# A two-layer hybrid diffusion backbone: attention by pairs of heads, and other places for modulation and stage ends

## The chip, the core and the metric

The kernel runs on one core of a Trainium2 chip. The metric is device time in microseconds (us) of one execution. Three runs gave 1413.24, 1419.32 and 1423.5 us; the median is 1419.32.

## What is computed

The reference is one inference step of two layers (`DEPTH`) over 128 context tokens and 256 latent tokens with 1024 channels. Cut to what matters:

```python
def _block(x, mod, lw, mix):
    g = lw['norm_g']
    h = _rms(x, g[0]) * (1 + mod[:, None, 1]) + mod[:, None, 0]
    y, aux = mix(h)
    x = x + mod[:, None, 2] * _rms(y @ lw['w_out'], g[1])
    h = _rms(x, g[2]) * (1 + mod[:, None, 4]) + mod[:, None, 3]
    f = jnp.square(jax.nn.relu(h @ lw['ffn_w1'])) @ lw['ffn_w2']
    x = x + mod[:, None, 5] * _rms(f, g[3])
    return x, aux
def _modulation(cond, w, b):
    m = jax.nn.silu(cond) @ w + b          # six vectors of 1024 for each layer
    return m.reshape(cond.shape[0], N_MOD, D_MODEL)
# mix: h @ w_in is cut into four groups of heads
#   A bidirectional RWKV-7 (a recurrence), B neighbourhood attention, C bidirectional HGRN2, D windowed attention with a sink
#   y = concat(A, B, C, D); attention for one query block:
    p = jax.nn.softmax(jnp.concatenate([s_loc, s_ctx], axis=-1), axis=-1)
    o = jnp.einsum('bhrcqak,brackhd->brcqhd', p_loc, vb) + jnp.einsum('bhrcql,blhd->brcqhd', p_ctx, cv)
...
```

B and D have four heads of 64 channels each. Context queries see context only, latent queries see latent and context.

## The kernel before

All 384 tokens lie in three tiles of 128 partitions, or, transposed, as 128 channels by 384 tokens. Weights come in units of 128x1024 (512 KB). A dense product is made in three passes over high and low halves (`hh`/`hl` of the activations, `wh`/`wl` of the weights; `dwh`/`dwl` are the same from a second pair of pools). ScalarE makes the high half by a cast (L330), VectorE the low half by a subtraction (L318).

The stages, in order: `start` (modulation vectors 0 and 1 of layer 0, the first norm), `mix` of layer 0 (29 units of w_in, then the four groups of heads), `wout` of layer 0, `ffn` of layer 0 (32 units of w1, 32 of w2), and the same three for layer 1. The modulation weights (`modw`) are summed by `mod_sums`: each 512 KB load holds two blocks of 128 rows, and a row of four narrow products goes to four column groups of 32 of the array. Layer 0's vectors 2, 4 and 3 are made during its `mix`, its vector 5 and those of layer 1 in its `ffn`. In `start` and `ffn` their weights go into four tiles `wm` from the POOL queue, in `mix` into the three `ws` slots that the projection uses, from the SP queue.

Within `mix` the four groups are generators. `merge` gives each a clock that starts at an offset and runs at a rate (`P`: 'ao', 'ar' for B, 'so', 'sr' for D, 'mo' = 60 and 'mr' = 7.5 for the late modulation) and always emits from the one whose clock is least. The framework then orders the instructions on each engine by a simulated timeline. Engines run their instructions in that order; the SP queue starts its transfers in that order, so a load whose slot is not free holds those behind it. The RWKV group inverts triangular matrices by small products and scans the chunks as a chain (its copies are on L1044); around the inverse SP moves data out and back (L954, L958, L970, L974). When all groups but RWKV are done, `wout_early` emits units 2, 3, 6, 7, 4, 5 of the output projection; units 0 and 1 need RWKV's result.

`attention(l, which)` works on one head at a time: three score products of 64 rows, maxima, exponentials with sums on ScalarE, transposes of the 384-wide weights, seven products with 64 moving columns (the values stream, the transposed weights are stationary), and a multiply by the reciprocal sums straight from PSUM (L318, 128x192). After two heads, three transposes bring their outputs to channels by tokens. `dense_end` ends a stage: its last units are multiplied tile by tile, so that the norm of a tile can run beside the next tile's products; `ntail` = 4 is the number of such units in `ffn`. `prepare` splits weights of the next stage beside it. `presplit` splits layer 1's w_in during layer 0's `ffn` and stores the low halves (POOL queue).

## Time and profile before

| | us |
|---|---|
| median of three runs | 1419.32 |
| the profiled execution | 1414.67 |
| its span on the core | 1412.6 |
| TensorE busy | 1290.0 (91%) |
| VectorE busy | 771.5 (55%) |
| ScalarE busy | 639.3 (45%) |
| mean granted TensorE clock | 0.948 |

The span is from the first to the last instruction; the rest of the profiled execution's time lies around it. Busy time is what an engine spent in instructions other than waits, branches and the issue of transfers. PE is TensorE, DVE VectorE, ACT ScalarE, SP and POOL queues. The granted clock is a share of 2.4 GHz; 0.5 means that the stretch ran at 1.2 GHz. From the timeline, the stages are: start to about 49 us, projection and head groups of layer 0 to about 390, output projection to 442.72 (first product of the feed-forward), feed-forward to 751.95, layer 1's groups from 764.88, its output projection to 1125.11, the last product at 1404.3.

### The profile page before, as it was taken

The page shows a single profiled execution, that of the slowest core. Times are in us where ns is not written, and L with a number is a line of the kernel's source. Part 1 is how long each engine was busy: PE and PEld are TensorE (multiplying, and loading weights), DVE is VectorE, ACT ScalarE, POOL GpSimd, SP SyncE. Part 2 cuts the span into 40 slices and gives each one's busy share as a digit, 9 for nine tenths or more (in the row PEclk, how much of TensorE's full clock was granted, in tenths as well). Part 3 has the DMA queues.
Part 4 walks back from the last instruction along what each step waited for, and adds up shares of the span by engine and source line. Part 5 has one row for each costly group of instructions (what it writes and reads, how often), then busy time and mean ns, then how long its engine had stood idle before and what let it go on. Part 6 is the DMA issues. An engine that isn't in the chain of part 4 may idle for free.

```text
span 1412.6 us, 21044 instructions
## 1 busy us (share of the span) xinstructions
PE 1290.0 (91%) x8294; PEld 1087.4 (77%) x8294; DVE 771.5 (55%) x1453; ACT 639.3 (45%) x1255; POOL 101.1 (7%) x181
## 2 busy tenths in 40 slices
PE   5898999899885999999997999879999699999997
PEld 1787778567765888887896888769876588999996
DVE  2497968724356445544534369984544643434443
ACT  4557624333355344444435579324544533333332
POOL 3000000000000122221100000000000000000000
PEclk9999998959997999999998999979999799999999
DMA  9432524721282699999832655117216345343411
GB/s 339 135 104 75 163 72 131 228 78 44 79 289 81 234 330 359 327 326 345 290 114 77 217 172 181 61 49 219 61 50 245 127 134 164 121 130 123 127 53 45
DMA packets 85427, 229.55 MB, mean 163 GB/s; under 512 B 24720, under 2 KB 27088, under 8 KB 85328
## 3 DMA queue, kind: packets, MB, share of 16 engines
q1 hardware_dynamic: 58688, 157.84, 34.4%
q0 software_dynamic: 14672, 52.99, 10.1%
q10 hardware_dynamic: 11968, 17.37, 3.8%
q8 instruction: 65, 1.06, 0.3%
q14 instruction: 34, 0.28, 0.1%
HBM read 206.90 MB, written 21.27 MB: 162 GB/s over the span
## 4 chain that ended last, share of the span: by engine, by line
PE 75%; DVE 9%; DMA 7%; ACT 6%; issue 2%; POOL 0%; ACTq 0%; DVEq 0%; POOLq 0%; SPq 0%
PE pd L333 36%; PE pm L333 19%; PE pr L333 17%; DVE mix L318 4%; DMA wm<-modw 2%; ACT mix L327 2%; PE pm L336 2%; DMA low<-wl 2%; ACT tmp L327 2%; DVE wl L318 1%; DMA ws<-modw 1%; ACT wh L330 1%; DMA wl<-low 1%; PE pr L336 1%; DVE mix L321 1%
## 5 line engine op out<-in xcount | busy, mean ns | idle before, releaser
L333 PE MATMUL pd<-hh,wh 128*128 128x384 f32 (+2 forms) x656 | 225.3, 344 | 15.2 <-ACT hh L330 10.2
L333 PE MATMUL pd<-hh,wl 128*128 128x384 f32 (+2 forms) x656 | 225.2, 344 | 8.5 <-DVE wl L318 5.6
L333 PE MATMUL pd<-hl,wh 128*128 128x384 f32 (+2 forms) x656 | 222.8, 340 | 0.5 <-DVE hl L318 0.5
L330 ACT CAST wh<-ws 128x1024 fp32r<-128x1024 f32 x121 | 126.4, 1047 | 164.6 <-PE pd L333 58.6
L318 DVE TENSOR_TENSOR wl<-ws,wh 128x1024 fp32r<-128x1024 f32 x92 | 112.3, 1221 | 97.7 <-ACT wh L330 61.0
L333 PEld LDWEIGHTS pd<-hh,wh 128*128 128x128 f32 x656 | 127.3, 195 | 24.0 <-ACT hh L330 11.3
L318 DVE TENSOR_TENSOR mix<-mix 128x384 f32<-128x384 f32 (+19 forms) x272 | 123.6, 468 | 28.1 <-ACT mix L330 13.3
L333 PEld LDWEIGHTS pd<-hh,wl 128*128 128x128 f32 x656 | 126.9, 194 | 15.5 <-DVE wl L318 7.4
L333 PEld LDWEIGHTS pd<-hl,wh 128*128 128x128 f32 x656 | 127.0, 194 | 2.5 <-DVE hl L318 1.6
L333 PE MATMUL pd<-hh,dwh 128*128 128x384 f32 (+2 forms) x368 | 123.3, 337 | 4.1 <-ACT hh L330 3.0
L327 ACT ACTIVATE mix<-mix 128x384 f32<-128x384 f32 (+4 forms) x188 | 107.1, 600 | 39.7 <-DVE mix L318 19.9
L333 PE MATMUL pd<-hl,dwh 128*128 128x384 f32 (+2 forms) x368 | 123.4, 335 | 0.3 <-DVE hl L318 0.3
L333 PE MATMUL pd<-hh,dwl 128*128 128x384 f32 (+2 forms) x368 | 122.9, 334 | 0.0
L318 DVE TENSOR_TENSOR dwl<-ws,dwh 128x1024 fp32r<-128x1024 f32 x44 | 53.9, 1224 | 68.3 <-ACT dwh L330 68.2
L330 ACT COPY mix<-pr 32x384 f32<-32x384 f32 (+7 forms) x136 | 42.0, 336 | 101.6 <-PE pr L333 64.1
L318 DVE TENSOR_TENSOR dwl<-dws,dwh 128x1024 fp32r<-128x1024 f32 x44 | 53.5, 1222 | 61.1 <-ACT dwh L330 59.6
L333 PE MATMUL pm<-mix,mix 128*128 128x64 f32 (+4 forms) x468 | 80.0, 319 | 6.8 <-ACT mix L330 3.6
L333 PE MATMUL pr<-dwh,f 128*128 128x512 f32 x252 | 80.4, 397 | 0.0
L333 PE MATMUL pm<-mix 128*128 128x128 f32 (+5 forms) x700 | 75.0, 266 | 4.3 <-DVE mix L318 3.0
L333 PE MATMUL pm<-dwh,f 128*128 128x512 f32 x252 | 78.7, 391 | 0.0
L333 PEld LDWEIGHTS pd<-hh,dwh 128*128 128x128 f32 x368 | 70.3, 192 | 7.4 <-ACT hh L330 3.6
L333 PE MATMUL pr<-mix,mix 128*64 128x64 f32 (+3 forms) x800 | 70.7, 230 | 3.5 <-DVE mix L1044 2.9
(211 smaller groups left out, 2300.6 us busy)
## 6 DMA issues: line engine op xcount, KB each, us to landing
ws<-win SPq DMA_DIRECT2D x87, 512.0 KB, 4.8
wm<-modw POOLq DMA_DIRECT2D x72, 512.0 KB, 7.5
dws<-w SPq DMA_DIRECT2D x64, 512.0 KB, 5.0
ws<-w SPq DMA_DIRECT2D x64, 512.0 KB, 4.1
low<-wl POOLq DMA_DIRECT2D x29, 512.0 KB, 7.0
wl<-low SPq DMA_DIRECT2D x29, 512.0 KB, 3.7
ws<-modw SPq DMA_DIRECT2D x24, 512.0 KB, 4.2
ws<-wout SPq DMA_DIRECT2D x14, 512.0 KB, 5.4
```

Of the source, the lines that this page charges most:

```text
L318: (eng or self.nc.vector).tensor_tensor(out, a, b, op=op)
L321: self.nc.vector.scalar_tensor_tensor(out, a, s, b, op0=op0, op1=op1)
L327: self.nc.scalar.activation(out, a, fn, **kw)
L330: self.nc.scalar.copy(out, a)
L333: self.nc.tensor.matmul(out, l, r, start=start, stop=stop)
L336: self.nc.tensor.transpose(out, a, self.ident[:k, :k])
```

## The change

In `attention`, two heads are done together, chosen so that they lie on partitions 0 to 63 and 64 to 127. Their score products alternate between the two row halves of the array, and go to separate PSUM banks. The weights are normalized (multiplied by the reciprocal sums) before they are transposed. The values are now stationary (64 columns) and the weights stream with 256 or 128 columns; the two heads write the two partition halves of one PSUM tile, which is already channels by tokens, so the transposes of z go. For D the order of heads becomes 0, 2, 1, 3; the rows of w_out are permuted on the host to fit. The mask of D is loaded once per pair.

Beside that: layer 0's `modw` loads of `start` go on SP and alternately into `wm` tiles and the weight slots; late modulation is not emitted before all units of w_in are; `wout` does unit 0 over all tiles and only unit 1 tile by tile; `ntail` is 6, and the two units more use `wm` tiles; presplitting begins later.

```diff
-        "wout": a["w_out"],
+        "wout": a["w_out"][:, np.concatenate([np.arange(768), _heads(768, (0, 2, 1, 3))])],
...
-P = {... 'mo': 60, 'mr': 7.5, 'ps': 7.2, 'po': 6, ...}
+P = {... 'mr': 2.5, 'ps': 7.4, 'po': 16, ...}
...
-        self.xs, self.xw, self.ntail = P['xw'], 4, 4
+        self.xs, self.xw, self.ntail = P['xw'], 4, 6
...
-        h, lo = self.slot("wh", F32R), self.slot("wl", F32R)
+        if own:
+            h, lo = (self.wmod.tile([128, 1024], F32R, name="wm", tag="wm") for _ in range(2))
+        else:
+            h, lo = self.slot("wh", F32R), self.slot("wl", F32R)
...
-            if self.wmod is not None:
+            q = self.nc.sync if l == 0 and ch < 5 else self.nc.gpsimd
+            if self.wmod is not None and (l or ch == 5 or u % 2):
                 w = self.wmod.tile([128, 1024], F32, name="wm", tag="wm")
-                q = self.nc.gpsimd
             else:
-                w, q = self.slot("ws", F32), self.nc.sync
+                w = self.slot("ws", F32)
...
     def attention(self, l, which):
...
+        for c in range(2):
+            heads = [2 * c + j if which == 0 else 2 * j + c for j in range(2)]
...
+                for j, (q, kt) in enumerate(qk):
+                    self.mm(pa[j][:, 0:T], q[:, 128 + t * 128:256 + t * 128], kt[:, 128:512])
...
+                nc.vector.reciprocal(r[:, j, 0:3], s[j][:, 2, 0:3])
+                self.ts(ex[j][1], ex[j][1], r[:, j, 0:1])
                 for t in range(2):
+                    self.ts(es[:, t], es[:, t], r[:, j, 1 + t:2 + t])
...
-                po = self.pw(3)[:, 0:192].rearrange("q (c v) -> q c v", c=3)
-                self.mm(po[:, 0], tp[0][:, 384:512], vs[0])
-                for t in range(2):
-                    for b in range(3):
-                        self.mm(po[:, 1 + t], tp[t][:, b * 128:b * 128 + 128], vs[1 + b] if b < 2 else cv, b == 0, b == 2)
+            po = self.pm()[:, 0:T]
+            for b in range(4):
+                for j in range(2):
+                    tp, hd = tps[j][1], heads[j]
+                    js = slice(j * 64, j * 64 + 64)
...
+                    if b < 3:
+                        self.mm(po[js, 128:T], v, tp[:, b * 256:b * 256 + 256], b == 0, b == 2)
+                    else:
+                        self.mm(po[js, 0:128], v, tp[:, 768:896])
...
-                self.tt(zb.ap(3, 2, 64)[:, :, j], po, rec[:, j].unsqueeze(2).broadcast_to([128, 3, 64]))
-                yield 3.0
-            rb.free()
-            ps = self.pm()[:, 0:T]
-            for t in range(3):
-                self.tr(ps[:, t * 128:t * 128 + 128], z[:, t * 128:t * 128 + 128])
...
     def dense_end(self, units, nxt, save, ahead=()):
-        w = [self.unit(src) for src, _ in units]
+        w = [self.fetch(src, i < len(units) - 4) for i, (src, _) in enumerate(units)]
...
     def wout(self, l):
-        yield from self.dense_end([self.wout_unit(l, n) for n in (0, 1)], (l, 3), None, [self.io["w1"][l, n] for n in range(P["na"])])
+        s, y = self.wout_unit(l, 0)
+        self.rows_product(self.acc, *y, self.unit(s), False, False)
+        yield 3.9
+        yield from self.dense_end([self.wout_unit(l, 1)], (l, 3), None, [self.io["w1"][l, n] for n in range(P["na"])])
...
         def mod(l, chunks):
+            while self.win_left:
+                yield 2.0
             for ch in chunks:
...
-            self.mix(l, [(P["mo"], P["mr"], mod(l, (2, 4, 3)), 0)] if l == 0 else [])
+            self.mix(l, [(0, P["mr"], mod(l, (2, 4, 3)), 0)] if l == 0 else [])
```

The order of instructions moves at three places that matter below. The first is the SP queue from layer 0's input projection (`win`) to the loads of `wout`; `inv` and `mix` are the moves around the RWKV inverse. Before:

```order
L370 DMA ws<-win 128x1024 x4
L544 DMA ws<-modw 128x2x512 x3
L954 DMA inv<-mix_344 32x24x32 x4
L544 DMA ws<-modw 128x2x512
L370 DMA ws<-win 128x1024 x2
L958 DMA mix_340<-inv 96x1024
L370 DMA ws<-win 128x1024 x3
L544 DMA ws<-modw 128x2x512 x12
L370 DMA ws<-wout 128x1024 x3
L970 DMA inv<-mix_340 96x1024
L370 DMA ws<-wout 128x1024 x2
L974 DMA mix_344<-inv 32x24x32 x4
```

and with the change:

```order
L370 DMA ws<-win 128x1024 x26
L957 DMA inv<-mix_344 32x24x32 x4
L961 DMA mix_340<-inv 96x1024
L370 DMA ws<-win 128x1024 x2
L547 DMA ws<-modw 128x2x512 x11
L973 DMA inv<-mix_340 96x1024
L547 DMA ws<-modw 128x2x512 x2
L977 DMA mix_344<-inv 32x24x32 x4
L547 DMA ws<-modw 128x2x512 x11
L370 DMA ws<-wout 128x1024 x5
```

The 24 `modw` loads that stood between `win` units stand behind the last of them, with two of the inverse's four moves among them, and ahead of `wout`.

The second is TensorE at the end of RWKV's chain in layer 0 (the shape at the end of a row is that of what is written; `pr` with 64x64 is the chain; 128x384 with `cst` and `lora` are the steps that form RWKV's result; 128x512 are products of the output projection). Before:

```order
L333 MATMUL pr<-mix_344,mix_340 64x64
L333 MATMUL pr<-mix_340,cst 128x384
L333 MATMUL pr<-mix_340,lora 128x384
L333 MATMUL pr<-wh,hh 128x512
L333 MATMUL pr<-wl,hh 128x512
...
L333 MATMUL pr<-mix_340,cst 128x384
L333 MATMUL pd<-wh,hh 128x512 x2
L333 MATMUL pm<-wh,hh 128x512 x3
L333 MATMUL pr<-wh,hh 128x512
L333 MATMUL pd<-wl,hh 128x512 x2
```

and with the change:

```order
L333 MATMUL pr<-mix_344,mix_340 64x64
L333 MATMUL pr<-mix_340,cst 128x384 x2
L333 MATMUL pr<-mix_344,lora 128x384
L333 MATMUL pr<-mix_340,cst 128x384 x2
L333 MATMUL pr<-mix_344,lora 128x384
L333 MATMUL pd<-dwh,hh 128x512 x2
L333 MATMUL pm<-dwh,hh 128x512 x3
L333 MATMUL pr<-dwh,hh 128x512
```

Before, 114 products of the output projection, of both kinds of units, stand behind the chain's last full round, 40 of them between the steps that form the result. Now 36 stand there, those of units 0 and 1, all behind these steps; the 78 others are ahead, between pieces of the chain.

The third is TensorE in an attention of layer 0, the products with the values. Before, between transposes of weights (L336):

```order
L333 MATMUL pr<-mix_344 64x64
L333 MATMUL pm<-mix_336,mix_340 128x64 x3
L336 MATMUL pm<-cst,mix_340 128x128 x3
L333 MATMUL pr<-mix_340,mix_344 64x64
L333 MATMUL pr<-mix_344 64x64
L333 MATMUL pr<-mix_340,mix_344 64x64
L333 MATMUL pm<-mix_340 128x64 x3
L333 MATMUL pm<-mix_336,mix_340 128x64
L333 MATMUL pm<-mix_336,mix_340 128x128
```

and with the change, beside the chain (`pr`):

```order
L333 MATMUL pr<-mix_344,mix_340 64x64
L333 MATMUL pm<-mix_340,mix_336 64x256
L333 MATMUL pm<-mix_336 64x256
...
L333 MATMUL pm<-mix_340,mix_336 64x128
L333 MATMUL pm<-mix_336 64x128
L333 MATMUL pm<-mix_340 64x256 x4
L333 MATMUL pm<-mix_340,mix_336 64x256 x2
L333 MATMUL pm<-mix_340 64x128 x2
L333 MATMUL pr<-mix_344 64x64
```

The 64-column products of one head have become 256- and 128-column ones, and those of two heads alternate.

## Rows read from the trace of the kernel before

**Rows 1.** Page, part 4: the chain that ended last, by engine.

```profile
PE 75%; DVE 9%; DMA 7%; ACT 6%; issue 2%; POOL 0%; ACTq 0%; DVEq 0%; POOLq 0%; SPq 0%
```

**Rows 2.** Stages: from:to, length, busy time by engine, granted clock, DMA share, GB/s.

```profile
0.00:49.00 49.00, 27.97 (x129) 11.39 (x129) 14.62 (x47) 20.84 (x45) 13.23 (x24) 1.00 0.80 294
160.00:180.00 20.00, 18.56 (x138) 14.29 (x137) 19.76 (x35) 12.81 (x20) 0.00 (x0) 1.00 0.40 132
200.00:230.00 30.00, 28.15 (x243) 21.75 (x242) 16.63 (x41) 10.04 (x30) 2.54 (x6) 0.77 0.49 135
282.00:328.00 46.00, 41.99 (x337) 33.09 (x339) 12.72 (x36) 17.18 (x49) 1.06 (x2) 0.55 0.27 79
328.00:390.00 62.00, 56.10 (x645) 44.85 (x641) 24.92 (x75) 19.88 (x73) 1.83 (x8) 1.00 0.18 59
390.00:443.00 53.00, 35.60 (x141) 27.62 (x142) 35.53 (x56) 31.45 (x62) 4.03 (x6) 0.82 0.70 246
443.00:752.00 309.00, 307.31 (x1642) 257.56 (x1642) 147.84 (x199) 132.86 (x191) 48.07 (x73) 0.99 0.75 266
1000.00:1085.00 85.00, 79.54 (x789) 62.28 (x789) 41.17 (x123) 36.83 (x119) 4.94 (x12) 0.98 0.32 105
```

**Rows 3.** Transfers of the stretch 0 to 40 us.

```profile
DMA packets 4315, 13.28 MB, mean 332 GB/s; under 512 B 735, under 2 KB 1119, under 8 KB 4314
```

**Rows 4.** TensorE in order of time, start: start, us, instruction, [idle before, releaser].

```profile
41.41 1.05 PE L333 MATMUL pd<-wm,cstat 128*32 128x512 f32 x4 [1.45 <-DMA wm<-modw]
...
48.91 0.62 PE L333 MATMUL pd<-hh,wh 128*128 128x384 f32 x2 [2.38 <-ACT hh L330]
```

**Rows 5.** Chain of waits in order of time, 200 to 450: start, us, what.

```profile
209.75 4.36 DMA ws<-modw
...
269.53 5.27 DMA ws<-modw
...
409.20 0.91 PE pd L333 x4
```

**Rows 6.** Groups of 49 to 282, TensorE: count, busy us, mean ns, idle before.

```profile
L333 PE MATMUL pd<-ws,cstat 128*32 128x512 f32 x96 | 20.6, 603 | 4.3 <-DMA ws<-modw 4.0
```

**Rows 7.** TensorE in order of time, in the two attention stretches.

```profile
350.67 1.13 PE L333 MATMUL pm<-mix,mix 64*128 64x384 f32 x4
351.73 0.33 PE L333 MATMUL pr<-mix 128*64 128x64 f32 x2
...
1015.35 1.55 PE L333 MATMUL pm<-mix 64*128 64x384 f32 x4
...
1020.71 0.88 PE L333 MATMUL pm<-mix,mix 128*128 128x64 f32 x6 [0.95 <-ACT mix L330]
...
1021.65 0.61 PE L336 MATMUL pm<-cst,mix 128*128 128x128 f32 x4
```

**Rows 8.** Groups of VectorE, shapes kept apart, whole span.

```profile
L318 DVE TENSOR_TENSOR mix<-pm,mix 128x192 f32<-128x192 f32 x16 | 5.7, 356 | 13.7 <-PE pm L333 13.6
...
L324 DVE TENSOR_SCALAR mix<-mix,prm 128x384 f32<-128x384 f32 x12 | 5.2, 433 | 1.7 <-ACT mix L327 1.6
```

**Rows 9.** SP's queue in order of time, 237 to 290.

```profile
237.71 35.68 SPq L544 DMA_DIRECT2D ws<-modw  x12
...
288.28 3.27 SPq L974 DMA_DIRECT2D mix<-inv  x4
```

**Rows 10.** TensorE in order of time, end of the output projection, layer 0.

```profile
389.06 0.29 PE L333 MATMUL pr<-mix,mix 128*64 128x64 f32 x4
...
435.32 1.97 PE L336 MATMUL pd<-cst,tmp 128*128 128x128 f32 x8 [10.99 <-DVE tmp L324]
...
442.72 0.79 PE L333 MATMUL pd<-hh,dwh 128*128 128x256 f32 x2 [2.73 <-ACT hh L330]
```

**Rows 11.** TensorE in order of time, end of the feed-forward, layer 0.

```profile
757.25 1.12 PE L336 MATMUL pm<-cst,tmp 128*128 128x128 f32 x4 [5.30 <-ACT tmp L327]
...
764.88 0.80 PE L333 MATMUL pd<-hh,wh 128*128 128x256 f32 x2 [3.95 <-ACT hh L330]
```

More of the change, by code (lines that the diff above doesn't have):

```diff
@@ L363, in unit, with fetch @@
         return self.fetch(src)
-    def fetch(self, src):
+    def fetch(self, src, own=False):
         low = None
@@ L1306, in attention @@
-                for t in range(2):
-                    for b in range(3):
-                        self.mm(po[:, 1 + t], tp[t][:, b * 128:b * 128 + 128], vs[1 + b] if b < 2 else cv, b == 0, b == 2)
-                tb.free()
-                self.tt(zb.ap(3, 2, 64)[:, :, j], po, rec[:, j].unsqueeze(2).broadcast_to([128, 3, 64]))
-                yield 3.0
-            rb.free()
-            ps = self.pm()[:, 0:T]
-            for t in range(3):
-                self.tr(ps[:, t * 128:t * 128 + 128], z[:, t * 128:t * 128 + 128])
@@ L1323, in attention @@
+            for tb, _ in tps:
+                tb.free()
+            self.y_block(2 + c if which == 0 else 6 + c, po)
+            yield 2.0
         for b in ((*self.nq, *self.nk, self.nv, self.ncv) if which == 0 else (*self.sq, self.sk, self.sv, self.scv)):
@@ L1716, in mod @@
         def mod(l, chunks):
+            while self.win_left:
+                yield 2.0
             for ch in chunks:
```

120 lines of the change are left out of this document (65 added, 55 removed).

## The prediction, on record before the changed kernel ran

> **What bounds the kernel now.** I first read the chain of waits by engine [rows 1]: TensorE holds 75% of the span, VectorE 9%, transfers 7%, ScalarE 6%. So time is won by less TensorE work, by fewer pauses of it, or by a higher granted clock. The table of stages [rows 2] says where each is possible. The feed-forward of layer 0 (443 to 752 us) keeps TensorE busy for 307.31 of 309 us: only fewer matmuls would shorten it, and the change takes none away there. The rest has slack. The start (0 to 49) has TensorE busy for 27.97 us and a transfer share of 0.80. From 200 to 230 the clock is 0.77 and VectorE is busy for only 16.63 us, while in the ordinary input-projection slice 160 to 180 VectorE is busy for 19.76 of 20 us, so that VectorE is the bound there. From 282 to 328 TensorE is busy for 41.99 of 46 us at a clock of 0.55: about half of that time is the low level (1.2 instead of 2.4 GHz). From 390 to 443, the end of the output projection, TensorE is busy for 35.60 of 53 us at 0.82. From 752 to 765 it stands still twice [rows 11]. Layer 1's attention stretch, 1000 to 1085, is nearly full on TensorE (79.54 of 85) with VectorE at 41.17.
>
> **The change, part by part.** The sum is made against the profiled execution, 1414.67 us; the median of the runs is 4.65 us above it. A gain is negative.
>
> *Start.* By 40 us 13.28 MB have moved [rows 3], the last modulation matmuls wait for their weights and run at 41.41, and the projection runs steadily from 48.91 [rows 4]. The new order on SP puts 14 modulation loads ahead of the first projection load and two more right behind it, into tiles of three pools instead of four tiles of one. The last sum needs 16 x 0.52 = 8.4 MB of these weights, 1.5 MB of x, and by my estimate 1 MB besides: 10.9 of the 13.28 MB, which at the mean of [rows 3], 332 GB/s, is there after 33 us plus some start-up. I take -6 (bounds 0 and -8; 0 if the loads come no earlier). The Trainium skill ("DMA: Bandwidth & Descriptors", Issuing engines are not separate DMA queues) says that the issuing engine changes nothing but issue time, so by it the move from POOL to SP is worth 0. That agrees with the full transfer engines here, and my 6 us come from the order of the bytes.
>
> *Late modulation.* 24 loads and 96 matmuls (20.6 us busy, 4.0 us of it preceded by waits for a load [rows 6]) lie among layer 0's projection units. SP issues in order: at 209.75 the chain stands 4.36 us for such a load, and at 269.53 another 5.27 us [rows 5]; behind the first wait the low clock of 200 to 230 follows. Now all 24 come behind the last projection load. The idle of 4 us goes, and of the 30 us at 0.77 some 6.5: together -10 (bounds -11 and 0). The 20.6 us of TensorE work itself moves and does not vanish: it comes back beside attention and the RWKV inverse, where TensorE has 4 us idle in 282 to 328 but much clock to regain. Queued behind the 11 loads is the reload of the inverse on SP (row L973 of the order), behind 13 its last return, and behind all 24 wout. Before, the last 12 late loads begin at 237.71, behind the last projection load, and that return is issued at 288.28 [rows 9]. At the rate of [rows 3] a load takes 1.6 us, so 13 of them pass by about 259 even if the projection's own loads end no earlier. So SP should not be what is late; the inverse itself is late next.
>
> *Clock of 282 to 328.* The clock fell after short pauses while the last late loads dripped in. 42 us of work at 0.55 would be 23 at full clock, so the ends are -20 and 0. With 24 units of matmuls placed just here the engine is fuller, but it depends on their loads: I take -6, nearer to 0 because I can't name a work that covers every pause.
>
> *Attention, TensorE.* Per pair of heads 14 value products with 64 columns go: 8 of them took 1.10 us (1020.71 to the end of the row behind), 0.115 to 0.14 each, so 1.6 us; and 3 transposes of a z tile (four took 0.61) [rows 7], 0.35. In their place stand 8 products that stream 256 or 128 columns. A 64-row score product of 384 columns costs about 0.32 us serially (four in 1.55), so 256 columns cost 0.21 and 128 cost 0.11: 0.75 us per head, 0.75 for the pair if the two column halves run at once, 1.5 if not. The scores of a pair, 4 x 0.32 + 2 x 0.11 = 1.5, fall to 0.75 likewise. The trace has a hint for overlap: where heads on different row halves met (350.67), four took 1.13 and not 1.55. So a pair saves 1.9 us, or 0.45 if all is serial; four pairs per layer: -7.6, or -1.8. At the low clock it would be double.
>
> The Trainium skill ("TensorEngine Tiling (Array Packing)", Key Properties) speaks against the change: it says that a change of tiling mode drains the engine. Here the 64-row block of 350.67 ends at 351.80 and the next product with another tile shape starts at 351.73, so no drain shows; the section "Stationary-Streaming Swap + Column Tiling" of that page names this very rearrangement for few columns. By the first rule the sum would lose the attention term, by the second it keeps it.
>
> *Attention, VectorE.* Per head one product out of PSUM goes (0.356 us), and normalizing adds two of 128x384 (0.433 each) and one of 128x128, which I put at 0.41 [rows 8]: +0.92 us per head, +7.4 us per layer, in line between the exponentials and the transposes. VectorE has room in 282 to 390 (37.64 of 108 us busy) and in 1000 to 1085, so most lies beside other work; if the RWKV chain's copies queue behind it, all of it counts. I take +2 in layer 0 and +2 in layer 1 (0 to +7.4 each).
>
> In both layers some of the TensorE saving is not on the path, since attention fills the pauses of a chain: -5 of 7.6 in layer 0 and -5 in layer 1.
>
> *End of the output projection, layer 0.* Behind the chain's last matmuls (389.06) 114 products of 512 columns stood at 0.23 us each (four in 0.91, [rows 5]); now 36 (8.3 us) stand there, and 78 (18 us) run inside the chain. That chain stretch has TensorE busy for 56.10 of 62 us, so of the 18 us some 6 fit in its pauses and 4 or so into what attention no longer takes: +8. Behind the chain the steps that form RWKV's two rows of y took until about 409 beneath the products; they are now exposed, and only then 8.3 us follow: 389 + 20 + 8 = 417 instead of the end of products at 424.3 (435.32 less 10.99 of idle, [rows 10]), and up to 8 us less where the steps no longer share VectorE with weight splits: -12. The norm then takes 424.3 to 442.72; it holds two short waits of splits, which move: -2. Sum -6 (bounds -14, and +10 if the exposed steps drop the clock for the products that follow). Layer 1 the same with fewer matmuls moved (132 to 108 behind the chain): -1 (-5 to +3).
>
> *End of the feed-forward, layer 0.* The last product ends at 751.95 (757.25 less 5.30), the first new one is at 764.88 [rows 11]: 12.9 us, and a low clock for 3 us behind. With six units tile by tile instead of four, a tile's products take half as long again, about 8.3 us, so the norm of tiles 0 and 1 ends beneath tile 2's products, and the first new products start on these. Left is 5 to 7 us: -7 (bounds -10 and -2). The last end gains nothing, as nothing follows but the last tile. Later presplitting and the permuted rows of wout cost nothing: the feed-forward's TensorE covers them with 307 of 309 us; without that cover a late load would cost about 5 us.
>
> Sum: -6 - 10 - 6 - 5 + 2 - 6 - 7 - 5 + 2 - 1 = -42, so 1373 us for an execution like the profiled one, and 1377 us with the median's 4.65 us.
>
> **Rivals.**
> *A: the halves don't overlap, and normalizing is in the way.* Then attention gives -1.8 and costs +7.4 per layer, instead of -5 + 2: 17 us worse, 1394. For it: the 0.32 us steps at 1015.35; against it: 1.13 at 350.67.
> *B: layer 0's mixing does not shorten.* The inverse and the chain set its end, not the projection, and the freed time becomes waiting for the late modulation, which has to run anyway. Its terms (-10 - 6 - 5 + 2 - 6 = -25) shrink to -5: 1397; with A's half in layer 1 too, 1406. For it: the chain of small products is serial and 20.6 us of work is put beside it.
> *C, slower: the block of 24 loads is exposed.* If the last return of the inverse (L977 in the order) is issued later than the 288.28 of before, the chain begins later by the difference. 24 loads at 1.6 us are 38 us; were all of it ahead of the chain, and TensorE at half clock for half of the chain stretch's 56.10 us, that is +38 + 28 against -6 and -10 of start and stalls and -14 of the rest: +36, 1455. With half of the stream and of the clock loss covered, +3, 1422. Without the gains of layer 0's mixing the other terms are -20, so it decides from about 20 us on: a return issued behind 308. Against it: the transfer engines are only at 0.18 to 0.27 in 282 to 390, so there is room for the loads.
> *D: the start gives nothing,* because transfers are full anyway: 6 us worse, 1383, inside the range.
>
> **Chances.** Forecast with D 0.52, A 0.16, B 0.14, C 0.10, and 0.08 that more clock comes back than I took (below 1350: the -20 and the -14 of the bounds). Range 1350 to 1412. Changes under 1% (14 us) can't be told from none here, as the runs shown spread by 10 us. Faster by over 1% means under 1405: the forecast, the low case, three quarters of A and half of B (both lie close to that bound), 0.79. Within 1%: what is left of A and B and a little of C, 0.12. Slower: C, 0.09.
>
> **What the changed profile would show.** Start: steady projection near 43 instead of 48.91. No wait for modulation weights before the last projection unit, and 200 to 230 at full clock. The reload L977 issued before 288. Score products of a pair within 0.1 us of each other, eight value products in about 1 us. VectorE's normalizing rows without a chain copy waiting behind. 36 products behind the chain, first feed-forward product near 405 instead of 442.72. A gap of 5 to 7 us where 12.9 stood at 752. The forecast is wrong if the clock from the end of the projection to the end of the chain stays near 0.55, or if the chain's first copy comes later than in the kernel before.

## The result, and the profile after

The changed kernel takes 1394.52 us in the median of four runs (1390.85 to 1396.76), the kernel before 1421.41 beside it. The ratio is 0.9842, with a 95% interval of 0.9805 to 0.9879: 1.6% faster, 22 to 27 us, where 42 were forecast. The profiled execution took 1390.85 us with a span of 1389.1, so it stands 23.8 us below the profiled one of before.

These are the stages of the changed kernel (columns as in [rows 2]), cut at the first projection product after the last wait of the start (44.5), the end of layer 0's projection (242.8), the first and the last copy of RWKV's chain (297.3, 380.5), the first product of the feed-forward (423.1), its last (742.5), layer 1's first (752.2) and its first chain copy (981.1):

```profile
0.00:44.50 44.50, 28.73 (x129) 12.71 (x129) 14.55 (x46) 21.05 (x45) 2.23 (x9) 0.88 0.88 323
44.50:242.80 198.30, 185.33 (x1254) 169.79 (x1258) 166.54 (x312) 107.86 (x198) 10.77 (x23) 0.94 0.27 80
242.80:297.30 54.50, 47.64 (x437) 26.34 (x440) 30.17 (x110) 25.27 (x82) 1.71 (x3) 0.94 0.75 233
297.30:380.50 83.20, 77.65 (x724) 58.56 (x724) 35.05 (x97) 27.63 (x78) 2.05 (x8) 0.94 0.38 121
380.50:423.10 42.60, 20.73 (x88) 14.18 (x88) 29.46 (x53) 26.52 (x59) 3.51 (x5) 0.79 0.60 219
423.10:742.50 319.40, 312.85 (x1650) 265.26 (x1650) 152.41 (x206) 137.27 (x202) 48.44 (x74) 0.97 0.75 265
742.50:752.20 9.70, 1.66 (x8) 1.04 (x8) 5.87 (x14) 6.93 (x20) 1.50 (x3) 0.69 0.32 108
752.20:981.10 228.90, 215.31 (x1615) 195.78 (x1616) 162.86 (x350) 126.06 (x259) 11.08 (x23) 0.94 0.46 145
```

The same cuts, and what each stage took in both kernels and in the runs of the next section. All are from the traces; "copies" are those of the chain, L1044 before and L1047 after. The last column goes from layer 1's first product to the first of its feed-forward.

| us | start | projection | to first copy | chain | to feed-forward | feed-forward | gap | layer 1 |
|---|---|---|---|---|---|---|---|---|
| before | 48.9 | 206.4 | 68.9 | 62.0 | 56.5 | 309.3 | 12.9 | 360.2 |
| after | 44.5 | 198.3 | 54.5 | 83.2 | 42.6 | 319.4 | 9.7 | 348.8 |
| after, again | 41.6 | 197.1 | 57.8 | 83.2 | 42.6 | 319.0 | 9.7 | 359.2 |
| x1 attention alone | 47.2 | 205.9 | 60.1 | 62.4 | 57.3 | 309.7 | 12.9 | 362.2 |
| x2 all but attention | 41.7 | 187.3 | 75.9 | 82.8 | 47.0 | 313.5 | 7.6 | 364.3 |
| x3 old late modulation | 41.3 | 207.9 | 67.5 | 60.2 | 54.7 | 312.6 | 7.3 | 361.1 |
| x4 old start | 47.8 | 198.1 | 51.1 | 83.2 | 43.0 | 315.5 | 9.8 | 353.7 |
| x6 tail of four | 44.5 | 195.7 | 50.7 | 83.4 | 42.5 | 313.1 | 12.9 | 356.5 |
| x9 modulation at rate 5 | 42.8 | 218.8 | 35.9 | 76.9 | 43.5 | 316.8 | 9.8 | 353.8 |
| x10 no weaving | 41.8 | 199.3 | 51.9 | 65.7 | 56.1 | 317.9 | 7.1 | 360.4 |
| z2 rate 5, no weaving | 42.8 | 218.6 | 31.3 | 66.4 | 57.3 | 315.7 | 7.6 | 360.7 |
| w1 rate 5, old presplit | 42.4 | 219.7 | 31.3 | 78.3 | 43.5 | 310.1 | 9.8 | 361.1 |

So before and after differ by -4.4, -8.1, -14.4, +21.2, -13.9, +10.1, -3.2 and -11.4 us. Two stages became longer: the chain, and the feed-forward. The -11.4 of layer 1 cannot be credited to the change: the second execution of the same program took 359.2 there, 1.0 less than the kernel before. In both executions TensorE does the same 1615 products up to the first copy of layer 1, at another clock. First the row of the repeat, to be held against the last row above (0.94):

```profile
751.00:988.50 237.50, 224.54 (x1615) 203.75 (x1616) 163.03 (x350) 125.99 (x258) 11.04 (x23) 0.89 0.44 139
```

So 8.6 us of difference lie in this stage alone, where TensorE's half clock fell in other places. Over a whole span, TensorE's busy time times (1 - granted clock), summed over slices of 4 us, is about 51 us in the kernel before, 53 after and 67 in the repeat: these traces show no fall.

The places of the forecast, in order of time. TensorE at the start. The longest wait for a modulation load behind the first ones is at 27.97, the last sums end at 38.0 (42.5 before), and the projection runs steadily from 44.48, against 48.91 in [rows 4]:

```profile
27.97 1.05 PE L333 MATMUL pd<-wm,cstat 128*32 128x512 f32 x4 [1.81 <-DMA wm<-modw]
...
44.48 0.61 PE L333 MATMUL pd<-hh,wh 128*128 128x384 f32 x2 [2.39 <-ACT hh L330]
```

SP's queue where it carries late modulation: the last return of the inverse (L977) is issued at 269.10, against 288.28 in [rows 9]:

```profile
211.40 48.93 SPq L547 DMA_DIRECT2D ws<-modw  x11
261.14 0.33 SPq L973 DMA_DIRECT2D inv<-mix  x1
...
269.10 4.87 SPq L977 DMA_DIRECT2D mix<-inv  x4
```

TensorE's waits for those loads, which were to go; the two longest. All such waits together are 5.4 us (4.0 in the repeat), no less than the 4.0 of [rows 6]:

```profile
248.02 1.92 PE L333 MATMUL pd<-ws,cstat 128*32 128x512 f32 x4 [2.34 <-DMA ws<-modw]
...
271.86 1.05 PE L333 MATMUL pd<-ws,cstat 128*32 128x512 f32 x4 [1.66 <-DMA ws<-modw]
```

Yet the clock in this stretch, from the end of the projection to the chain's first copy, is 0.94 (242.8 to 297.3 above). It was 0.71 before, and is 0.85 in the repeat:

```profile
255.30:324.20 68.90, 60.46 (x425) 40.52 (x424) 30.42 (x98) 25.37 (x79) 1.06 (x2) 0.71 0.51 158
238.70:296.50 57.80, 52.32 (x437) 28.30 (x440) 30.17 (x111) 25.46 (x82) 1.71 (x3) 0.85 0.70 220
```

Why it holds there, these traces alone don't tell.

Two heads' value products (a column half each, 128 rows by 64 columns) in layer 1, which [rows 7] could not show, as their rows of TensorE in order of time:

```profile
989.83 0.43 PE L333 MATMUL pm<-mix,mix 128*64 128x256 f32 x1
989.84 0.43 PE L333 MATMUL pm<-mix 128*64 128x256 f32 x1
990.10 0.38 PE L333 MATMUL pm<-mix,mix 128*64 128x256 f32 x1
990.11 0.38 PE L333 MATMUL pm<-mix 128*64 128x256 f32 x1
990.32 0.38 PE L333 MATMUL pm<-mix,mix 128*64 128x256 f32 x1
990.32 0.38 PE L333 MATMUL pm<-mix 128*64 128x256 f32 x1
```

They start in pairs, within 0.01 us, and one pair follows the other after 0.21 to 0.27 us. Each such product has two rows in the trace: a layer has 8 heads with 3 products of 256 columns, 24 in all, and its trace (970 to 1050) two groups of 24 rows, of which one is shown below. The dense products, on `F32R` operands, have one row each. So the eight value products of a pair are 16 rows; here they take 1.74 us:

```profile
L333 PE MATMUL pm<-mix,mix 128*64 128x256 f32 x24 | 5.4, 392 | 0.0
...
1013.00 1.74 PE L333 MATMUL pm<-mix 128*64 128x256 f32 x16
```

The score products do the same on the row halves where two heads meet: four rows in 0.92 us, against 1.55 in [rows 7]. In layer 1 this changes little: the groups of its 48 score rows add up to 16.3 us busy, against 17.0 before, some of them at half clock (572 ns in the mean of the largest group, 509 before). The product behind the four, of another tile shape, starts before their end:

```profile
306.36 0.92 PE L333 MATMUL pm<-mix 64*128 64x384 f32 x4
307.20 0.50 PE L333 MATMUL pr<-mix 128*64 128x64 f32 x6
```

VectorE's normalizing, by groups (half of them; the others have means of 413 and 304 ns): 0.41 and 0.28 us where [rows 8] gave 0.433 and the prediction took 0.41, so two of the one and one of the other are 1.1 us per head.

```profile
L324 DVE TENSOR_SCALAR mix<-mix 128x384 f32<-128x384 f32 x18 | 6.7, 411 | 0.0
...
L324 DVE TENSOR_SCALAR mix<-mix 128x128 f32<-128x128 f32 x9 | 2.5, 279 | 0.2
```

TensorE at the end of layer 0's output projection, answering [rows 10]: after the steps that form RWKV's result it waits 7.08 us for the last weights and casts, does 36 products, and waits 8.13 for the norm; the first feed-forward product is at 423.11.

```profile
397.65 1.22 PE L333 MATMUL pd<-dwh,hh 128*128 128x512 f32 x2 [7.08 <-ACT dwh L330]
...
416.06 1.97 PE L336 MATMUL pd<-cst,tmp 128*128 128x128 f32 x8 [8.13 <-DVE tmp L324]
...
423.11 0.80 PE L333 MATMUL pd<-hh,dwh 128*128 128x256 f32 x2 [3.07 <-ACT hh L330]
```

And at the end of its feed-forward, answering [rows 11]: pauses of 2.97 and 5.10 in place of 5.30 and 3.95, the whole gap 9.7 in place of 12.9.

```profile
745.44 0.66 PE L336 MATMUL pr<-cst,tmp 128*128 128x128 f32 x4 [2.97 <-DVE tmp L324]
...
752.21 0.79 PE L333 MATMUL pd<-hh,wh 128*128 128x256 f32 x2 [5.10 <-ACT hh L330]
```

### The profile page after: what moved, and what is told of

Read it like the earlier page. It is cut to its first block, busy times and chain, and to the rows that moved or that the text cites. A ratio compares the mean times of both kernels' runs of the same rounds, so it can differ in the third digit from the quotient of the medians.

```text
span 1389.1 us, 20850 instructions
## 1 busy us (share of the span) xinstructions
PE 1265.2 (91%) x8174; PEld 1065.9 (77%) x8174; DVE 785.1 (57%) x1509; ACT 639.2 (46%) x1255; POOL 89.6 (6%) x165
## 4 chain that ended last, share of the span: by engine, by line
PE 49%; DVE 9%; issue 6%; DMA 5%; ACT 4%; POOL 1%; SPq 0%; DVEq 0%; ACTq 0%; POOLq 0%
PE pd L333 24%; PE pr L333 12%; PE pm L333 11%; DVE mix L318 4%; DMA low<-wl 2%; ACT tmp L327 2%; DMA ws<-w 2%; ACT mix L327 1%; PE pm L336 1%; DVE tmp L321 1%; DVE wl L318 1%; DMA wl<-low 1%; DMA dws<-w 1%; ACT wh L330 1%; PE pd L336 1%
## 5 line engine op out<-in xcount | busy, mean ns | idle before, releaser
L333 PE MATMUL pd<-hl,wh 128*128 128x384 f32 (+2 forms) x640 | 218.6, 342 | 0.4 <-DVE hl L318 0.4
L318 DVE TENSOR_TENSOR mix<-mix 128x384 f32<-128x384 f32 (+19 forms) x288 | 134.6, 483 | 45.2 <-ACT mix L330 22.5
L333 PE MATMUL pd<-hh,dwh 128*128 128x384 f32 (+2 forms) x384 | 130.0, 341 | 8.4 <-ACT hh L330 6.7
L333 PEld LDWEIGHTS pd<-hh,wl 128*128 128x128 f32 x640 | 124.2, 194 | 10.4 <-issue 3.8
L333 PE MATMUL pd<-hl,dwh 128*128 128x384 f32 (+2 forms) x384 | 130.7, 341 | 0.7 <-DVE hl L318 0.6
L333 PE MATMUL pd<-hh,dwl 128*128 128x384 f32 (+2 forms) x384 | 130.2, 339 | 0.0
L327 ACT ACTIVATE mix<-mix 128x384 f32<-128x384 f32 (+4 forms) x188 | 106.9, 600 | 26.4 <-DVE mix L318 12.9
L333 PE MATMUL pr<-mix,mix 128*64 128x64 f32 (+3 forms) x1024 | 88.3, 238 | 9.3 <-DVE mix L318 6.3
L318 DVE TENSOR_TENSOR dwl<-dws,dwh 128x1024 fp32r<-128x1024 f32 x43 | 52.6, 1224 | 67.5 <-ACT dwh L330 67.5
L333 PEld LDWEIGHTS pr<-mix,mix 128*64 128x64 f32 (+3 forms) x1024 | 74.2, 149 | 20.3 <-issue 8.8
L333 PE MATMUL pm<-mix 128*32 128x32 f32 (+7 forms) x840 | 84.6, 271 | 2.1 <-DVE mix L318 1.3
L333 PEld LDWEIGHTS pd<-hh,dwh 128*128 128x128 f32 x384 | 75.5, 198 | 11.7 <-ACT hh L330 7.8
L333 PEld LDWEIGHTS pd<-hl,dwh 128*128 128x128 f32 x384 | 76.1, 198 | 2.9 <-DVE hl L318 1.5
L330 ACT COPY mix<-pr 64x128 f32<-64x128 f32 (+7 forms) x136 | 42.2, 336 | 75.0 <-PE pr L333 45.4
```

Of the source, the lines that this page charges most:

```text
L318: (eng or self.nc.vector).tensor_tensor(out, a, b, op=op)
L327: self.nc.scalar.activation(out, a, fn, **kw)
L330: self.nc.scalar.copy(out, a)
L333: self.nc.tensor.matmul(out, l, r, start=start, stop=stop)
```

## The experiments

Ratios are to the kernel before on the same chip, with 95% intervals. Most differ by little more than these, so the stages of the table say more than the medians do.

**x1: the attention alone, in the kernel before.**

```diff
-    def attention(self, l, which):   # one head at a time
+    def attention(self, l, which):   # by pairs of heads, as in the change
-        "wout": a["w_out"],
+        "wout": a["w_out"][:, np.concatenate([np.arange(768), _heads(768, (0, 2, 1, 3))])],
```

> The kernel before with only the new attention (pairs of heads, values stationary, weights normalized first, permuted rows of wout). Theory 1 (the halves run at once, saving 1.9 us of TensorE a pair, partly off the path, normalizing mostly covered): 5 to 10 us faster than before. Theory 2 (normalizing on VectorE is in the way and eats the saving): 0 to 10 us slower. Theory 3 (TensorE is the bound wherever attention runs, so the saving counts whole): 14 to 18 us faster.

1406.53 against 1423.48; 0.9874 (0.9809 to 0.9938), so 9 to 27 us faster. Theory 2 is out; the interval holds theory 3 and the upper end of theory 1. By the stages layer 0 is 9.9 us shorter up to its feed-forward: 8.8 in the stretch to the chain's first copy, where the clock also is 0.86 in place of 0.71, and 1.7 in the start, where there is no attention. The profiled execution was the slowest of the four (1413.28): it is 7.5 us ahead of the kernel before at layer 1's feed-forward, and 1.1 at the end.

**x2: all but the attention.**

```diff
+    def attention(self, l, which):   # the old one, and the old rows of wout
```

> The changed kernel with the old attention and the old rows of wout; all else as changed. Theory 1: 5 to 10 us slower than the changed kernel (about 1400 to 1405). Theory 2: no slower, or a few us faster. Theory 3: 14 to 18 us slower. If the attention's gain is larger here than alone, the late modulation and wout in the chain have made TensorE the bound there.

1414.98; 0.9918 (0.9877 to 0.9960). The rest of the change is worth 0.8%, some 11 us less than the whole (3 to 19), which fits theories 1 and 3 and not 2. Up to layer 0's feed-forward the rest gives -8.0, and with the -9.9 of x1 that makes about -18 of the -19.6 measured: the parts add up. So about half of that gain is attention, which the forecast gave 6 of 42.

**x3: late modulation as before, the rest changed.**

```diff
-            while self.win_left:
-                yield 2.0
-P = {... 'mr': 2.5, ...}
+P = {... 'mo': 60, 'mr': 7.5, ...}
```

> The changed kernel with the late modulation emitted as before (from its old clock, among the projection units). Theory M1 (the work only moved: the projection ends some 12 us earlier, the chain of RWKV takes that much longer beside 24 loads and their 20.6 us of TensorE): within 4 us of the changed kernel, the chain's first copy near 315 to 320 instead of 297.32 and its last within 4 us of 380.5. Theory M2 (the move is a net gain as predicted, about 10 us of stalls and low clock): 6 to 12 us slower, low clock again near 215 to 228. Theory M3 (the move hurts, since the chain stands on the end's path): 4 to 10 us faster.

1402.23; 0.9831 (0.9757 to 0.9906), the same as the changed kernel in the median, and the chain's copies come where theory M1 has them (316.7 and 376.9). The two ratios leave some 12 us either way, so the medians alone don't exclude M2. And M1's reason is not the one. The projection and the stretch behind it take 275.4 us, as before (275.3), against 252.8 in the changed kernel; and half clock stands there again:

```profile
249.20:316.70 67.50, 61.69 (x454) 37.19 (x454) 39.50 (x136) 29.47 (x92) 1.06 (x2) 0.75 0.54 163
```

What it loses there it has again later. At this late rate most of the early units of the output projection are emitted too late to come into the chain: 24 of their products stand in it, in place of 108. The chain takes 60.2 us in place of 83.2, the part behind it 54.7 in place of 42.6, and the feed-forward with its gap 319.9 in place of 329.1.

**x4: the start's loads as before.**

```diff
+            if self.wmod is not None:
+                w = self.wmod.tile([128, 1024], F32, name="wm", tag="wm")
+                q = self.nc.gpsimd
+            else:
+                w, q = self.slot("ws", F32), self.nc.sync
```

> The changed kernel with the modulation loads of the start as before (POOL queue, four wm tiles, one by one). Theory S1 (the order of bytes is worth what the trace shows at the steady projection, 44.48 against 48.91): 4 to 5 us slower than the changed kernel, and the projection steady near 49. Theory S2 (transfers or VectorE take it back within the projection): within 2 us, the end of the projection unmoved.

1396.78; 0.9800 (0.9740 to 0.9860). The projection is steady at 47.8 and ends at 245.9, against 238.7 to 242.8 in the runs with the new start and the same middle. At the first feed-forward product it is 423.2 against 423.1 and 422.3, and 416.7 in x6, whose code is the changed kernel's up to there. What the start gives is there up to the end of the projection, 3 to 7 us; behind it, it is within what executions differ by, and the medians do not show it.

**x10: no output projection inside the chain.**

```diff
-            if then and not any(c[1] for c in clock):
+            if then and not clock:
```

> The changed kernel with the early units of the output projection emitted only after RWKV's chain, so that 114 of its products stand behind the chain in either layer instead of 36 (layer 0) and 108 (layer 1). Theory W1 (the gain of layer 0 comes from these products running inside the chain: 42.6 us from the chain's last copy to the first feed-forward product, against 54 to 57 in the runs where 114 stand behind it): layer 0 about 10 us longer at its end, the chain's end some 3 to 5 us earlier, in all 5 to 9 us slower than the changed kernel. Theory W2 (weaving only moves work): within 3 us.

1396.15; 0.9809 (0.9740 to 0.9878): W2 by the stages, though the medians leave W1 up to 6 us. What the chain gains, the part behind it loses:

```profile
293.00:358.70 65.70, 58.58 (x646) 44.47 (x642) 28.36 (x91) 22.27 (x72) 2.05 (x8) 0.92 0.34 113
358.70:414.80 56.10, 36.14 (x167) 27.87 (x167) 36.12 (x57) 32.13 (x66) 3.51 (x5) 0.87 0.58 213
```

Chain 65.7 and 56.1 behind it, against 83.2 and 42.6 (both 0.92 to 0.94 and 0.79 to 0.87 in clock): 17.5 us cheaper, 13.5 dearer. TensorE is busy for 58.58 of the 65.70 us, and with the 78 products for 77.65 of 83.20: its pauses go from 7.1 to 5.6 us, so of the 18 us of products 1.6 found room. In the 7.1 us it waits mostly for the chain's own steps on other engines (2.7 us for VectorE's copies of L1047, 2.4 for POOL, 2.0 for ScalarE). The weight splits of these products lie in the chain too (VectorE 35.05 us busy against 28.36); no run separates what they delay from what the products delay.

x10 against x3 shows the late modulation by itself: neither has the 78 products in the chain, and the feed-forward begins at 414.8 and at 431.6. By the stages the new place is worth 17 us up to there; the medians differ by 0.2%, with 1% either way.

**x9: late modulation among the projection units, but at a rate of 5.**

```diff
+P = {... 'mo': 60, 'mr': 5, ...}
```

> The changed kernel with the late modulation among the projection units as before but with a rate of 5 instead of 7.5, which is early enough for 108 products of the output projection to be ahead of the chain's end, as in the changed kernel. Theory W1 (place of the modulation is worth nothing by itself; what it did was to let the output projection be emitted early): as fast as the changed kernel within 4 us, the chain to first feed-forward product 42 to 46 us. Theory M2 (keeping it out of the projection is itself worth about 10 us): 8 to 12 us slower than the changed kernel, with a wait for a modulation load and low clock in the projection.

1388.69; 0.9765 (0.9686 to 0.9843): no slower than the changed kernel, so keeping the loads out of the projection is worth nothing by itself, and M2 is out. Projection and the stretch to the first copy take 254.7 us, like the 252.8 of the changed kernel. That projection is 20 us longer, and the stretch 19 us shorter, though it now runs at 0.62:

```profile
261.60:297.50 35.90, 30.70 (x285) 21.52 (x285) 18.21 (x61) 18.41 (x55) 0.53 (x1) 0.62 0.46 138
```

The half clock there follows a pause in which TensorE has nothing left but the inverse, whose return from SP it waits for:

```profile
271.27 1.48 PE L333 MATMUL pr<-mix,mix 32*32 32x32 f32 x24 [3.95 <-DMA mix<-inv]
```

**x6: a tail of four units.**

```diff
-        self.xs, self.xw, self.ntail = P['xw'], 4, 6
+        self.xs, self.xw, self.ntail = P['xw'], 4, 4
```

> The changed kernel with four units instead of six done tile by tile at the end of the feed-forward. Theory T1 (as predicted, the gap at the end of layer 0's feed-forward shrinks by the longer tile): gap 12 to 13 us instead of 9.7, 3 to 4 us slower than the changed kernel. Theory T2 (the two units more cost something of their own, since the stage from the first feed-forward product to layer 1's first is 329 us in the changed kernel and 322 before): that stage 322 us or less, so as fast or faster.

1395.51; 0.9810 (0.9738 to 0.9882). The gap is 12.9 us again, so the longer tail is worth 3.2 there (T1); from the last modulation sum to the last product the feed-forward takes 65.4 us, about as in the changed kernel (66.8 and, repeated, 65.6), and 61.1 before; feed-forward and gap are 326.0 us together, not the 322 of T2. So T2 is out: the longer feed-forward has another cause.

**x8: the value products head by head.**

```diff
-            for b in range(4):
-                for j in range(2):
+            for j in range(2):
+                for b in range(4):
```

> The changed kernel with the value products of a pair issued head by head instead of alternating. Theory H1 (the two column halves run at once only when they alternate): eight products of a pair take about 1.5 us instead of 0.85, 16 us x 0.04 a pair, in all 3 to 5 us of TensorE more, of which little reaches the end. Theory H2 (the halves overlap whatever the order, or never do): the eight take the same time in both orders.

One run, 1397.46. The number "16 us x 0.04" in that text is a slip; 0.75 us a pair was meant. The text counts rows: the eight products of a pair are 16. Here they are head by head, to be held against the 1.74 us above, where they alternate:

```profile
1014.54 2.65 PE L333 MATMUL pm<-mix 128*64 128x256 f32 x16
```

From start to start, over the 64 rows of layer 1 wherever one follows another without a break, it is 0.169 us head by head and 0.116 alternating; for those of 256 columns alone 0.183 and 0.123, where 0.21 is one after the other. So the halves run at once where they alternate, and two heads still overlap somewhat where they don't: H1, with about 3 us a layer. One run doesn't show so little in the time.

**z1: the changed kernel again.** No edit.

> The changed kernel once more, beside the two that follow: how much stages of one program differ between executions. If the places of half clock are set by the program, each stage is within 2 us of the first profile (projection end 242.8, first chain copy 297.3, first feed-forward product 423.1, layer 1's first product 752.2, second layer's feed-forward 1101.0); if they fall where chance puts them, the stages differ by 4 to 8 us each and the ratio stays near 0.984.

1394.40; 0.9830 (0.9775 to 0.9884). Layer 0 repeats within 3.3 us in each stage, the second dip of the clock at the start of the feed-forward too; layer 1 up to its chain differs by 8.6. So both: some places of half clock came again, others did not. And 3.3 us is no bound: x6, with the same code that far, reaches its feed-forward 6.4 us earlier.

**z2: rate 5 and no weaving.**

```diff
+P = {... 'mo': 60, 'mr': 5, ...}
+            if then and not clock:
```

> The changed kernel with both: late modulation among the projection units at a rate of 5, and the early units of the output projection only behind the chain. Theory W2 (running the output projection inside the chain only moves work; the place of the modulation loads decides whether the clock holds before the chain): as fast as the run with the rate of 5 alone, within 4 us (about 0.975 of before), layer 0's chain 62 to 66 us, its end 54 to 57. Theory W1: 6 to 10 us slower than that run.

1391.03; 0.9816 (0.9747 to 0.9884). Chain 66.4, behind it 57.3; with x9's 76.9 and 43.5 that is 10.5 cheaper and 13.8 dearer. Here the two chains ran at different clocks, x9's at 1.00 and this one at 0.91:

```profile
297.50:374.40 76.90, 72.80 (x725) 56.11 (x725) 33.86 (x95) 28.59 (x84) 3.44 (x9) 1.00 0.25 82
292.70:359.10 66.40, 58.43 (x647) 45.89 (x647) 27.29 (x89) 23.27 (x78) 2.42 (x9) 0.91 0.17 55
```

By an estimate from these rows (66.40 x 0.09) 6 of the 7 us between 10.5 and x10's 17.5 are the clock's. W2 again by the stages; in time the difference from x9 (0.5%, with 1% either way) cannot be told from none, nor from W1.

**z3: the last eight loads held back.**

```diff
             for ch in chunks:
+                while ch == chunks[-1] and self.win_left:
+                    yield 2.0
                 yield from self.mod_chunk(l, ch)
+P = {... 'mo': 60, 'mr': 3.5, ...}      # and no weaving
```

> Late modulation at a rate of 3.5 among the projection units but its last chunk of eight loads held back until all units of w_in are emitted, and the output projection only behind the chain. Theory C1 (what costs at the chain's start is the half clock after a wait of TensorE for the inverse's transfer, 12.9 us of it in the run with the rate of 5; matmuls held back for that wait keep the clock): no half clock from 260 to 300, the first chain copy near 285, 8 to 12 us faster than the run with the rate of 5. Theory C2 (the inverse and its transfers set the chain's start, whatever the clock): first chain copy within 4 us of 297, time within 4 us of that run.

1401.84; 0.9866 (0.9814 to 0.9919). The first copy comes at 295.0, and the clock from the end of the projection to it is 0.76. Theory C1 is out: the held products ran (258.78 to 281.20), and the clock fell all the same. By C2 the first copy should be within 4 us of 297, which it is; the time is not, it is slower by about 1%, of which the feed-forward (318.8 us) and layer 1's chain (69.8, and 57.8 to 64.4 in the other runs) are part. What sets the chain's start, the inverse or its clock, is not settled.

**w1: rate 5 and the old presplitting.**

```diff
-P = {... 'ps': 7.4, 'po': 16, ...}
+P = {... 'mo': 60, 'mr': 5, 'ps': 7.2, 'po': 6, ...}
```

> The run with the rate of 5 (late modulation among the projection units, output projection inside the chain) with the presplitting of layer 1's w_in at its old offset and rate. Theory P1 (the later presplitting still runs when the last units of w2 are split, and VectorE waits there for its stores): from the last modulation sum to the last product of the feed-forward 61 to 62 us as in the kernel before, not 67.5, and no wait of VectorE for a store there; 5 us faster than that run, about 0.973 of before. Theory P2 (the longer stretch is that of six units done tile by tile, or of the clock): 65 us or more, and the time within 2 us of that run.

1392.50; 0.9840 (0.9809 to 0.9870). P1 for the mechanism: from the last modulation sum to the last product 61.9 us, against 67.5 in x9 and 61.1 in the kernel before. In the changed kernel VectorE waits for stores of the presplit low halves (`low<-wl`) in this very stretch, one after the other:

```profile
696.43 1.23 DVE L318 TENSOR_TENSOR wl<-ws,wh 128x1024 fp32r<-128x1024 f32 x1 [1.39 <-DMA low<-wl]
...
703.33 1.22 DVE L318 TENSOR_TENSOR wl<-ws,wh 128x1024 fp32r<-128x1024 f32 x1 [1.19 <-DMA low<-wl]
...
710.23 1.23 DVE L318 TENSOR_TENSOR wl<-ws,wh 128x1024 fp32r<-128x1024 f32 x1 [1.51 <-DMA low<-wl]
```

With the old offset the last such wait is 44 us before this stretch begins (663.5):

```profile
619.51 1.23 DVE L318 TENSOR_TENSOR wl<-ws,wh 128x1024 fp32r<-128x1024 f32 x1 [3.27 <-DMA low<-wl]
```

TensorE then pauses for ScalarE, twice in the changed kernel:

```profile
701.13 0.44 PE L333 MATMUL pd<-hh,dwh 128*128 128x384 f32 x1 [0.99 <-ACT tmp L327]
...
707.43 0.44 PE L333 MATMUL pd<-hh,wh 128*128 128x384 f32 x1 [1.80 <-ACT tmp L327]
```

All eleven traces with the later presplitting have such pauses in this stretch (1.1 to 4.4 us) and take 63.3 to 67.5 us for it; the three with the old one (before, x1, w1) have none and take 61.1 to 61.9. So it costs 2 to 6 us; that the one wait leads to the other is read from w1, where both are gone. But this doesn't show in the median, and no kernel of these beats the changed one by more than its interval.

## Why the prediction was right, and where it was not

The direction and the range were right, and the size was 1.6 to 1.9 times too large. By stages, forecast and measured: the start -6 and -4.4; projection to first copy, with layer 0's attention, -19 and -22.5; the chain +8 and +21.2; behind it -14 and -13.9; the feed-forward 0 and +10.1; the gap -7 and -3.2; layer 1 -4 and -11.4, or -1.0 in the repeat. So two terms failed, and attention was read wrongly.

*The step that failed most: the output projection inside the chain.* The text put 78 products (18 us) into the chain and took "+8" for them, since 6 us of pauses and 4 us left by attention would hold the rest. x10 against the changed kernel measures +17.5, nearly the whole of it. TensorE's pauses there were waits for the chain's own steps, and the products filled 1.6 us of them. The other half, -14 behind the chain, came out at -13.5 to -13.9. So this term is about +4, not -6, and with rate 5, where the clocks differ, it is -3; it is nothing that the medians can see. The first feed-forward product came at 423.11, not near 405; that sign did not follow from the text's own terms either, which give 442.72 - 31 = 412.

*Later presplitting "costs nothing".* It costs 2 to 6 us at the end of layer 0's feed-forward (w1). TensorE's 307 of 309 us was no cover: VectorE waits for the stores while it should split the last units for that same TensorE, which then pauses. Another 5 us of the stage's +10.1 are a second dip of the clock near its start: from its first product to its first modulation sum it takes 37.4 to 37.6 us in both executions, in x8, x10 and z3, but 32 to 33 in the kernel before and in the other eight runs. Why those five have it was not tried.

*Late modulation and the clock: right in sum, not by the part named.* The terms -10 and -6 were for projection and the stretch behind it; with attention's share these stages gave -22.5, of which x1 puts 9.3 down to attention and x2 12.1 to the rest. x10 against x3 gives -17 for the move alone, up to the feed-forward, near the -16 of these terms. But the waits for loads did not go (5.4 us against 4.0). What came back is the clock between projection and chain: 0.71 before, 0.94 and 0.85 after. And x9 shows that the loads need not leave the projection: earlier among its units does as well. What hurt was that the loads came late (the last 12 from 237.71 to 273, [rows 9]): z2 and x3 both have them among the units and no 78 products in the chain, and with the rate of 5 the first copy comes at 292.7, with 7.5 at 316.7. The text's "about half of that time" for a clock of 0.55 is a slip, as 0.55 means nine tenths at the low level; its sum goes by the 0.55.

*Attention: too small, by two wrong readings.* Forecast -6, measured 9 to 27 us alone and some 11 in the rest of the change. The text priced rows as products, and each product is two rows. A pair's 14 old value products are 28 rows, 3.2 to 3.9 us at its own 0.115 to 0.14, not 1.6; the eight new ones take 1.74, not 0.75. By an estimate from these rows, values and transposes of z save 7 to 10 us a layer, not 4.8. The scores, for which 3 us a layer were meant, gave 0.7 in layer 1, somewhat more at one clock. And the hint of overlap at 350.67 was none. That row merges two of 384 columns and two of 128, as the groups of 350.7 to 351.7 in the kernel before show:

```profile
L333 PE MATMUL pm<-mix,mix 64*128 64x384 f32 x2 | 0.9, 534 | 0.0
L333 PE MATMUL pm<-mix,mix 64*128 64x128 f32 x2 | 0.4, 270 | 0.0
```

At 0.21 us less for each of 128, 1.55 becomes 1.13 with no overlap at all. So that the halves do overlap was right, but not for this reason. Normalizing came as priced, 1.1 us per head. How much of the saving is on the path stays open: x1 gained 8.8 us in the stretch to the first copy, and its clock there (0.86 for 0.71) would be worth 12, by length times (1 - clock), an estimate from the rows.

*The start.* -4.4 at the steady projection and -7.3 in the repeat, for -6; right in mechanism, but x4 cannot find it behind the projection.

*The feed-forward's end.* -3.2 for -7 (9.7 us; 7.1 to 7.6 in x2, x3, x10, z2 and z3, whose tails are the same six units; what makes that difference was not tried). The norm's second transposes stand at 745.44, behind the last product (742.5), not beneath the third tile's products.

*Layer 1.* -3 and -1 were forecast, and two executions of one program differ by 10.4 us there. No size can be given.

*The rivals.* A (halves that do not overlap) is refuted by the pairs of starts; that its 1394 is the measured median is chance. B's 1397 is also nearer to the result than the forecast's 1377, and up to the chain's last copy layer 0 gained only 5.7 us (386.2 to 380.5), of which 4.4 is the start. But B's reason does not hold: the inverse and the chain did not set that end. The chain's first copy came 26.8 us earlier (324.2 to 297.3), and without the products in the chain (x10) its last one comes at 358.7. C needed L977 behind 308; it was issued at 269.10. The test named for the forecast's failure, a chain that begins later or at 0.55, did not occur; the failure came in the chain itself, for which no test was named.

The Trainium skill ("TensorEngine Tiling (Array Packing)", Key Properties) says that a change of tiling mode drains the engine. No idle time for it shows in these rows: the score products of 306.36 end at 307.28, and the product of another tile shape starts at 307.20. The first pair of value products at 989.83 is longer than the next (0.43 against 0.38 us), but so is a first product of another kind without a change of tile shape (0.42 against 0.34 at 248.83 in the kernel before); a price below 0.1 us stays open.

## What to carry to other kernels

Pauses within a serial chain are not free room: count a block of work put beside such a chain at its full length until a trace shows less. Before a row's time is taken as the price of a product, count the rows and the products, and look at what a merged row holds. When loads that feed small products must be spread, spread them early and let them end together with the work that covers them, because a late drip moves all that follows it: here the chain's first copy came at 316.7 us with it and at 292.7 with earlier loads. Before reading a gain from one profile, profile one program twice: here one stage differs by 9 us with nothing changed.

## What the runs showed of the hardware

Half clock comes back in many of the same places of layer 0 in both executions of one program, twice around the start of its feed-forward (412 to 429 and 436 to 446, at 0.51; in the repeat 411 to 428 and 435 to 445, at 0.50). Yet layer 1's mixing up to its chain ran at 0.94 in one and 0.89 in the other. Less idle time did not mean more clock: about 51 us lost in the kernel before, 53 and 67 in the changed one, 80 in x1. A product on `F32` operands has two rows in the trace, one on `F32R` operands one (24 products of 256 columns in a layer, 48 rows). Value products that write different column halves started within 0.01 us of each other. Heads issued one after the other still overlapped somewhat (0.183 us from start to start of 256 columns, where 0.21 would be one after the other, and 0.123 where they alternate).
